# A decoder block on one core: the second FFN projection wholly by seven half-size products, with the sums of its weights begun earlier and the last row's squares summed on VectorE

## The chip, the cores and the metric

The kernel runs on one core of a Trainium2 chip. A core has five engines, each with its own instruction queue that is worked off in order: TensorE (PE; its weight loads are listed as PEld), VectorE (DVE), ScalarE (ACT), GpSimd (POOL) and SyncE (SP, which here only issues DMAs). They wait for each other by semaphores. Matmul results stand in eight PSUM banks of 128 partitions x 512 fp32 words. The metric is the device time of one launch in microseconds; lower is better.

## The reference

One layer of a decoder block, batch 1, 512 tokens, model width 1024, everything in fp32. The first half (a gated MLP mixer and a sparse attention, merged and projected) leaves the residual stream `x`; the change lies in the second half and the final norm:

```python
    h2 = rms_norm(x, norm2_g) * (1.0 + scale2) + shift2
    f_g, f_u = jnp.split(h2 @ w_ffn_in, 2, axis=-1)
    x = x + gate2 * ((jax.nn.silu(f_g) * f_u) @ w_ffn_out)
    return x
...
    return rms_norm(x, final_norm_g)
```

`w_ffn_out` is 2816 x 1024: 22 k tiles of 128 rows, two halves of 512 columns.

## The kernel before

**Precision.** An fp32 product is made of three fp32r matmuls (`mm3`, L51 to 55): each operand is split into `hi` (a rounded copy, made by ScalarE, L112 for weights and L1579 for activations) and `lo` (the rest, made by VectorE, L116 and L1583), and hi·hi, hi·lo and lo·hi are added in PSUM.

**Order.** The order of instructions on every engine is the order in which the program emits them. Weights come through one stream: SyncE loads a chunk into one of three `raw` buffers, `prep` splits it into one of three `hi`/`lo` pairs, and `get(i)` sees to it that the chunks up to two ahead are prepared before chunk i is used. So ScalarE's `hi` of chunk i+2 waits until TensorE is through with chunk i-1.

**Stages.** Towards the end of the span they are: projection B (`opt_b` over `W_PB`, eight chunks, with `o_step` called after each), the output projection O (`oprod`, seven half-size products, then direct matmuls over `W_O`), the second norm and its transposes, the first FFN projection (a direct part, then `sprod`, twenty rounds `q` of seven products), and the second FFN projection, which is what the change is about.

**The second FFN projection, called Z here.** Its output (512 x 1024) is four quadrants of 256 tokens x 512 columns, each in two PSUM banks (`Z[0]` to `Z[3]`). Twenty of the 22 k tiles are cut into two halves of ten (`KZ`) and done by Strassen's scheme in Winograd's form: seven products instead of eight, `zprod`, in the order A11, S1, S2, A12, S3, A22, S4. Each takes an activation operand (A.. are parts of the activations `gz`; S1 = A21-A22, S2 = A11-S1, S3 = S2-A22, S4 = A12-S2, formed in place by VectorE in `a_sum`, split by `a_hi` and `a_lo` into `za`) and a weight operand (quarters of `w_ffn_out`, or one of four sums of quarters, `wsum` 1 to 4). A product is five chunks of two k tiles: per chunk and per 128 tokens (`e`) six matmuls of 512 columns. The lists handed to `zprod` hold, for each chunk, the small jobs that are emitted between `get` and the chunk's matmuls. `z_copy` and `z_out` copy quadrants by ScalarE, `z_add` adds a kept copy by VectorE.

The two k tiles left over (`KC`, tiles 20 and 21) are added directly after the fifth product: their activations are split into `gs` (`g_hi`, `g_lo`, L1792 and L1795), and two chunks `W_FO` are multiplied into all four quadrants, 48 matmuls of 512 columns.

**The weight sums.** `wsum` 1 to 4 are made in DRAM by DMAs that GpSimd issues, some of them adding into their target (L305), some copying (L307). They are cut into five row chunks of six steps each, and the steps are dealt out by `wstep` (L317): a ScalarE copy and a GpSimd copy of one column (L323, L324) hold the step's DMAs back to that place, then they are issued, each after those before it on the same rows have landed. `wstep` is called twice in each of the twenty rounds q; every fourth call does nothing.

**The end.** During the last two products the finished quadrants are scaled by the gate, added to the residual and squared: `resid_v` (two VectorE passes, L1238 and L1239; ScalarE sums the squares, L1240), `scale_g` (VectorE, L1724), `row_rstd` (VectorE reduces, L1247, GpSimd raises to -1/2, L1248) and `finish` (scaling shared by VectorE and ScalarE, L1728 and L1727, then the store). The last product's third to fifth chunk are done for token tile 0 first and then for token tile 1 in two column halves, so that most of the end overlaps matmuls.

## Time and profile before

| | us |
|---|---|
| median of 3 runs | 823.71 (823.35 to 824.3) |
| the profiled execution | 824.09 |
| its span, first to last instruction | 822.3 |
| TensorE busy in the span | 807.8 |
| VectorE busy | 683.2 |
| ScalarE busy | 427.6 |
| GpSimd busy | 156.3 |

The granted TensorE clock was 0.998 of full speed in that execution. A matmul's listed duration is a modelled one that overlaps with the next matmul's; the pace at which matmuls are issued is read from the starts of many of them. Likewise two VectorE rows can overlap a little, so what one costs in a row of them is the distance of their starts.

### The profile page before, as it was taken

To read this page: it belongs to the slowest core of one execution; us is meant where nothing else is said; L and a number is where in the kernel's file an instruction comes from. 1 tells how busy PE (TensorE), PEld (TensorE's weight loads), DVE (VectorE), ACT (ScalarE), POOL (GpSimd) and SP (SyncE) were. 2 spreads that over 40 slices of the span, in tenths; PEclk is the share of its full clock that TensorE was granted. 3 is DMA by queue.
4 is the path that set the end of the run, shared out by engine and by line. 5 is a ranking of instruction groups with operands and counts; after the bars stand their busy time and mean duration, and the time that the engine had idled before them with its cause. 6 is when DMAs were issued, how large, how long until landed. Compare 5 with 4: busy or idle time off the path is not lost.

```text
span 822.3 us, 12898 instructions
## 1 busy us (share of the span) xinstructions
PE 807.8 (98%) x4912; PEld 721.2 (88%) x4912; DVE 683.2 (83%) x1163; ACT 427.6 (52%) x758; POOL 156.3 (19%) x171
## 2 busy tenths in 40 slices
...
GB/s 295 311 210 119 103 179 78 106 101 89 113 135 201 174 185 103 26 111 257 201 124 20 186 26 149 198 268 230 296 224 246 200 220 173 231 205 203 180 128 128
DMA packets 107197, 138.46 MB, mean 168 GB/s; under 512 B 6480, under 2 KB 77136, under 8 KB 106976
## 3 DMA queue, kind: packets, MB, share of 16 engines
...
q0 software_dynamic: 9584, 27.07, 14.1%
...
q10 hardware_dynamic: 720, 0.82, 0.3%
...
## 4 chain that ended last, share of the span: by engine, by line
PE 53%; DVE 17%; DMA 5%; ACT 2%; issue 2%; POOL 0%; POOLq 0%; DVEq 0%; ACTq 0%
PE R L53 8%; PE R L54 8%; PE R L55 8%; DMA mraw<-in_w_ada_dram 4%; DVE acc L177 3%; PE pfo L55 3%; PE pfo L54 3%; PE pfo L53 3%; DVE lo L116 2%; DVE sco L720 2%; DVE m L716 2%; PE pb L53 2%; PE pb L55 2%; PE pb L54 2%; PE po L54 2%
## 5 line engine op out<-in xcount | busy, mean ns | idle before, releaser
L112 ACT ACTIVATE hi<-raw 128x1024 fp32r<-128x1024 f32 (+2 forms) x103 | 107.0, 1040 | 107.7 <-PE pb L54 27.5
L116 DVE TENSOR_TENSOR lo<-raw,hi 128x1024 fp32r<-128x1024 f32 (+2 forms) x67 | 81.1, 1215 | 30.5 <-ACT hi L112 30.3
L116 POOL TENSOR_TENSOR lo<-raw,hi 128x1024 fp32r<-128x1024 f32 x29 | 73.2, 2529 | 127.9 <-ACT hi L112 122.2
L53 PE MATMUL pb<-h,hi 128*128 128x512 f32 (+1 forms) x192 | 74.6, 388 | 0.0
L55 PE MATMUL pb<-h,lo 128*128 128x512 f32 (+1 forms) x192 | 73.9, 385 | 0.0
L54 PE MATMUL pb<-h,hi 128*128 128x512 f32 (+1 forms) x192 | 73.9, 385 | 0.0
L54 PE MATMUL pfo<-lo,za 128*128 128x512 f32 (+1 forms) x146 | 56.5, 387 | 1.0 <-DVE lo L116 1.0
L55 PE MATMUL pfo<-hi,za 128*128 128x512 f32 (+1 forms) x146 | 56.2, 385 | 0.0
L53 PE MATMUL pfo<-hi,za 128*128 128x512 f32 (+1 forms) x146 | 56.2, 385 | 0.0
L177 DVE SCALAR_TENSOR_TENSOR acc<-mraw,cols,acc 128x512 f32<-128x512 f32 x49 | 40.1, 818 | 17.4 <-DMA mraw<-in_w_ada_dram 16.4
L53 PE MATMUL R<-tb,sx 128*128 128x256 f32 x160 | 45.2, 282 | 0.3 <-ACT R L1683 0.3
L1248 POOL TENSOR_TENSOR sm<-sm,mhalf 128x1 f32<-128x1 f32 x8 | 5.3, 663 | 209.8 <-DVE sm L1247 209.8
L54 PE MATMUL R<-tb,sx 128*128 128x256 f32 x160 | 45.1, 282 | 0.0
L55 PE MATMUL R<-tb,sx 128*128 128x256 f32 x160 | 45.0, 281 | 0.0
L55 PE MATMUL R<-tb,lo 128*128 128x256 f32 x160 | 44.8, 280 | 0.0
L53 PE MATMUL R<-tb,hi 128*128 128x256 f32 x160 | 44.8, 280 | 0.0
L54 PE MATMUL R<-tb,hi 128*128 128x256 f32 x160 | 44.6, 279 | 0.0
L55 PEld LDWEIGHTS pb<-h,lo 128*128 128x128 f32 x192 | 36.0, 188 | 7.3
L54 PEld LDWEIGHTS pb<-h,hi 128*128 128x128 f32 x192 | 36.0, 188 | 6.9
L53 PEld LDWEIGHTS pb<-h,hi 128*128 128x128 f32 x192 | 36.0, 188 | 6.9
L324 POOL COPY sm<-sm 128x1 f32<-128x1 f32 x30 | 18.9, 632 | 106.0 <-ACT sm L323 105.9
L54 PE MATMUL pav<-lo,h 128*128 128x256 f32 x128 | 35.8, 279 | 0.0
(380 smaller groups left out, 2666.7 us busy)
## 6 DMA issues: line engine op xcount, KB each, us to landing
...
```

Of the source, the lines that this page charges most:

```text
L53: T.matmul(o, wh, rh, start=start, stop=False, **kw)
L54: T.matmul(o, wh, rlo, start=False, stop=False, **kw)
L55: T.matmul(o, wlo, rh, start=False, stop=stop, **kw)
L112: A.activation(hi[:, :m], e["raw"][:, :m], AF.Copy)
L116: e["lo"].tensor_sub(lo[:, :m], e["raw"][:, :m], f(hi[:, :m]))
L177: V.scalar_tensor_tensor(o, w, cs[:, j:j + 1], o, op0=OP.mult, op1=OP.add)
L324: P.tensor_copy(t, t)
L716: V.max(m8s[i], sco[i])
L720: V.match_replace(out=sco[i], in_to_replace=m8s[i], in_values=sco[i], imm_value=TAKEN)
L1248: P.tensor_tensor(r2[:, tk:tk + 1], r2[:, tk:tk + 1], mhalf[:, :1], op=OP.pow)
```

## The change

All 22 k tiles of Z go through the seven products, in halves of eleven. A product is now five chunks of two k tiles and a sixth chunk of one (256 KB, half the columns to split, half the matmuls). The direct part (`W_FO`, `gs`) is gone. The operand parts for the sixth chunk are 128 x 256 pieces (`zl`, two places used in turn). The sums in DRAM have a sixth row chunk of half the size, so 36 steps in place of 30; eight calls of `wstep` are added ahead of the twenty rounds: five in the later `o_step` of projection B, three in O. `final_norm_g` is loaded into another buffer, its load emitted with the fifth product's first chunk instead of its last. At the end, three chunks (five k tiles) instead of three chunks of two are done in the split order. Row 0's scaling is done by ScalarE alone, and for the last quarter the squares are summed by VectorE in one pass that also adds the sums made before (GpSimd adds those up ahead of it).

```diff
--- before.py
+++ after.py
@@ -266,12 +266,11 @@
     W_F = [group(w_ffn_in, c, where=wh) for c in (0, DFF)]
     st["limit"] = len(stream)
 
-    KZ = ([0, 1, 2, 3, 4, 5, 6, 7, 12, 13], [8, 9, 10, 11, 16, 17, 18, 19, 14, 15])
-    KC = [20, 21]
-    NZ = 5
+    KZ = ([0, 1, 2, 3, 4, 5, 6, 7, 12, 13, 20], [8, 9, 10, 11, 16, 17, 18, 19, 14, 15, 21])
+    NZ = 6
 
     dram = ctx.enter_context(tc.tile_pool(name="dram", bufs=1, space=bass.MemoryType.DRAM))
-    wsum = {n: dram.tile([NZ * 256, 512], F32, name=f"wsum{n}") for n in (1, 2, 3, 4)}
+    wsum = {n: dram.tile([11 * 128, 512], F32, name=f"wsum{n}") for n in (1, 2, 3, 4)}
     W_Z = {}
 
     def add_z(key):
@@ -281,24 +280,22 @@
                 src, k0, c0 = wsum[key], 2 * c, 0
             else:
                 src, k0, c0 = w_ffn_out, KZ[key[0]][2 * c], key[1] * 512
-            W_Z[key].append(add_w(src, [k0, k0 + 1], c0, 512))
-
-    for key in ((0, 0), 1, 2, (1, 0), 3):
+            W_Z[key].append(add_w(src, [k0, k0 + 1][:1 + (c < 5)], c0, 512))
+
+    for key in ((0, 0), 1, 2, (1, 0), 3, 4, (1, 1)):
         add_z(key)
-    W_FO = [add_w(w_ffn_out, KC, 512 * h, 512) for h in range(2)]
-    for key in (4, (1, 1)):
-        add_z(key)
 
     def wsum_steps():
 
         def step(c, *moves):
-            o = slice(256 * c, 256 * c + 256)
+            n_ = 256 if c < 5 else 128
+            o = slice(256 * c, 256 * c + n_)
 
             def fn():
                 for n, add, src in moves:
                     if isinstance(src, tuple):
                         k = KZ[src[0]][2 * c] * 128
-                        src = w_ffn_out[k:k + 256, 512 * src[1]:512 * src[1] + 512]
+                        src = w_ffn_out[k:k + n_, 512 * src[1]:512 * src[1] + 512]
                     else:
                         src = wsum[src][o]
                     if add:
@@ -319,7 +316,8 @@
 
         fn = wsteps.pop(0) if wsteps else None
         if fn:
-            t = sm[:, 20 + len(wsteps):21 + len(wsteps)]
+            k = 20 + sum(w is not None for w in wsteps)
+            t = sm[:, k:k + 1]
             A.activation(t, cols[:, 58:59], AF.Copy)
             P.tensor_copy(t, t)
             fn()
@@ -1217,6 +1215,8 @@
     def o_step():
         for fn in O_STEPS.pop(0):
             fn()
+        if len(O_STEPS) < 5:
+            wstep()
 
     mbank[0] = 5
     o_issue("B11", "B12", "B22")
@@ -1404,15 +1404,18 @@
     o_m("S3")
     keep(O, 3, None)
     o_w("B22", "B22")
+    wstep()
     oprod(1, "S2", "T2", False)
     o_m("S4")
     o_sub("B11", "B21", "B11")
     seed(O, OB, 2, 1)
     oprod(0, "A12", "B21", False)
+    wstep()
     o_w("T4", "B11")
     o_m("A22")
     ensure(W_O[1])
     oprod(2, "S3", "T3", False)
+    wstep()
     keep(O, 2, "acc")
     oprod(1, "S4", "B22", False)
     ensure(W_O[2])
@@ -1550,7 +1553,7 @@
 
 
 
-    za = {}
+    za, zl = {}, []
     ZA = {"A11": ("S2_0", "E2", "F0"), "S1": ("E4", "S2_4", "S2_6"), "S2": ("E3", "E7", "S2_7"),
           "A12": ("E0", "E1", "S2_2"), "S3": ("S2_0", "E2", "F0"), "A22": ("E4", "S2_4", "S2_6"),
           "S4": ("E3", "E7", "S2_7")}
@@ -1560,14 +1563,20 @@
 
     def a_part(name, c):
         kh, th = AT_[name]
-        t = gz[((0, 1, 3), (2, 4, 3))[kh][c]]
-        if c == 2:
-            t = t[:, 2 * kh:2 * kh + 2]
+        t = gz[((0, 1, 3, 5), (2, 4, 3, 5))[kh][c]]
+        if c >= 2:
+            n = 4 - c
+            t = t[:, n * kh:n * kh + n]
         return t[:, :, th * 256:(th + 1) * 256]
 
     def a_hi(key, c):
-        h = ZA[key][c]
-        if c == 2:
+        h = (ZA[key] + (None,))[c]
+        if c == 3:
+            if not zl:
+                zl.append(base.tile([128, 2, 2, 1, 256], F32R, name="zl", tag="S2_3", bufs=1))
+            t = zl[0][:, ("A11", "S1", "S2", "A12", "S3", "A22", "S4").index(key) % 2]
+            t = (t[:, 0], t[:, 1])
+        elif c == 2:
             t = (base if h[0] == "S" else ffn[0]).tile([128, 2, 2, 256], F32R, name="za", tag=h, bufs=1)
             t = (t[:, 0], t[:, 1])
         elif h[0] == "S":
@@ -1733,12 +1742,12 @@
     Z, ZB = {}, ((4, 7), (0, 1), (2, 3), (5, 6))
 
     def zmm(o, ka, c, e, w, cc, start, stop):
-        ah, al = za[ka, c // 2]
+        ah, al = za[ka, c // 2 if c < 5 else 3]
         wh, wl = w
-        for j in range(2):
-            k_ = 2 * (c % 2) + j
+        for j in range(1 + (c < 5)):
+            k_ = 2 * (c % 2) + j if c < 5 else 0
             a = tuple(t[:, k_, e * 128:(e + 1) * 128] for t in (ah, al))
-            mm3(o, a, (wh[:, j, cc], wl[:, j, cc]), start and j == 0, stop and j == 1, skip_group_check=True)
+            mm3(o, a, (wh[:, j, cc], wl[:, j, cc]), start and j == 0, stop, skip_group_check=True)
 
     ALL = slice(0, 512)
 
@@ -1780,46 +1789,31 @@
         while left:
             left.pop(0)()
 
-    fng, gs = [], []
+    fng = []
 
     def load_fng():
-        fng.append(base.tile([128, D], F32, name="fng", tag="S2_3", bufs=1))
+        fng.append(ffn[0].tile([128, D], F32, name="fng", tag="E0", bufs=1))
         P.dma_start(fng[0], rows_bcast(final_norm_g, D))
 
-    def g_hi():
-        t = ffn[0].tile([128, 2, 2, S], F32R, name="gs", tag="E0", bufs=1)
-        gs.extend((t[:, 0], t[:, 1]))
-        A.activation(gs[0], gz[5], AF.Copy)
-
-    def g_lo():
-        V.tensor_sub(gs[1], gz[5], f(gs[0]))
-
-    zprod(0, "A11", (0, 0), True, [[outs_left, hi_("S1", 0)], [lo_("S1", 0), hi_("S1", 1)],
-                                   [lo_("S1", 1), hi_("S1", 2), sm_("S2", 1), lo_("S1", 2)],
-                                   [sm_("S2", 2), hi_("S2", 0)], [lo_("S2", 0), hi_("S2", 1)]])
+    zprod(0, "A11", (0, 0), True, [[outs_left, hi_("S1", 0)], [lo_("S1", 0), hi_("S1", 1), hi_("A11", 3)],
+                                   [lo_("S1", 1), lo_("A11", 3), hi_("S1", 2), sm_("S2", 1)],
+                                   [lo_("S1", 2), sm_("S1", 3), sm_("S2", 2), hi_("S2", 0)],
+                                   [sm_("S2", 3), lo_("S2", 0), hi_("S1", 3)], [lo_("S1", 3), hi_("S2", 1)]])
     z_copy(1, 0, -1.0)
-    zprod(3, "S1", 1, True, [[lo_("S2", 1), hi_("S2", 2), sm_("S4", 0), lo_("S2", 2)], [sm_("S4", 1), hi_("A12", 0)],
-                             [sm_("S4", 2), lo_("A12", 0)], [hi_("A12", 1)],
-                             [lo_("A12", 1), hi_("A12", 2)]])
+    zprod(3, "S1", 1, True, [[lo_("S2", 1), hi_("S2", 2), sm_("S4", 0)], [lo_("S2", 2), sm_("S4", 1)],
+                             [sm_("S4", 2), sm_("S4", 3), hi_("A12", 0)], [lo_("A12", 0), hi_("A12", 1)],
+                             [lo_("A12", 1), hi_("A12", 2)], [lo_("A12", 2)]])
     z_out(3)
-    zprod(1, "S2", 2, False, [[lo_("A12", 2), sm_("S3", 0)], [sm_("S3", 1)], [sm_("S3", 2), hi_("S3", 0)],
-                              [lo_("S3", 0), hi_("S3", 1)], [lo_("S3", 1), hi_("S3", 2)]])
+    zprod(1, "S2", 2, False, [[hi_("S2", 3), sm_("S3", 0)], [lo_("S2", 3), sm_("S3", 1)], [sm_("S3", 2), sm_("S3", 3)],
+                              [hi_("S3", 0)], [lo_("S3", 0), hi_("S3", 1)], [lo_("S3", 1), hi_("A12", 3)]])
     z_copy(2, 1, -1.0)
-    zprod(0, "A12", (1, 0), False, [[lo_("S3", 2), hi_("A22", 0)], [lo_("A22", 0), lambda: z_add(1, 3, V.tensor_add)],
-                                    [hi_("A22", 1)], [lo_("A22", 1), hi_("A22", 2)], [lo_("A22", 2)]])
-    zprod(2, "S3", 3, False, [[hi_("S4", 0)], [lo_("S4", 0), hi_("S4", 1)], [lo_("S4", 1), hi_("S4", 2)],
-                              [lo_("S4", 2), g_hi], [g_lo, load_fng]])
+    zprod(0, "A12", (1, 0), False, [[lo_("A12", 3), hi_("S3", 2)], [lo_("S3", 2), lambda: z_add(1, 3, V.tensor_add)],
+                                    [hi_("A22", 0)], [lo_("A22", 0), hi_("A22", 1)], [lo_("A22", 1), hi_("A22", 2)],
+                                    [lo_("A22", 2)]])
+    zprod(2, "S3", 3, False, [[hi_("S3", 3), load_fng], [lo_("S3", 3), hi_("S4", 0)], [lo_("S4", 0), hi_("S4", 1)],
+                              [lo_("S4", 1), hi_("S4", 2)], [lo_("S4", 2), hi_("A22", 3)], [lo_("A22", 3)]])
     z_out(2)
     z_add(3, 2, V.tensor_sub)
-
-
-    for h in range(2):
-        hi, lo = get(W_FO[h])
-        for tk in range(4):
-            o = (Z[h] if tk < 2 else Z[2 + h])[tk % 2]
-            for j in range(2):
-                mm3(o, tuple(t[:, j, tk * 128:(tk + 1) * 128] for t in gs), (hi[:, j], lo[:, j]), False, True,
-                    skip_group_check=True)
 
 
     sq = []
@@ -1834,16 +1828,16 @@
         while sq:
             sq.pop(0)()
 
-    zprod(2, "A22", 4, False, [[res_(0, 0)], [sq_, res_(1, 0)], [sq_, res_(2, 1)], [sq_, res_(3, 1)], [sq_]])
+    zprod(2, "A22", 4, False, [[res_(0, 0)], [sq_, res_(1, 0)], [sq_], [res_(2, 1)], [sq_, hi_("S4", 3)], [lo_("S4", 3)]])
 
     def done(tk):
         row_rstd(tk)
         finish(tk)
 
-    zprod(1, "S4", (1, 1), False, [[res_(2, 0)], [sq_, res_(3, 0)]])
+    zprod(1, "S4", (1, 1), False, [[res_(3, 1)], [sq_, res_(2, 0)], [sq_, res_(3, 0)]])
     last = bank(7, "pfo")
     A.activation(last[:, :256], Z[1][1][:, 256:], AF.Copy)
-    ids = W_Z[1, 1][2:]
+    ids = W_Z[1, 1][3:]
     ch = [get(i, 2 - k) for k, i in enumerate(ids)]
     sq_()
     done(2)
@@ -1853,7 +1847,7 @@
             c = ALL if z is None else slice(256 * z, 256 * z + 256)
             o = Z[1][0] if z is None else (Z[1][1][:, :256], last[:, :256])[z]
             for n_, w in enumerate(ch):
-                zmm(o, "S4", 2 + n_, tk, w, c, False, n_ == 2)
+                zmm(o, "S4", 3 + n_, tk, w, c, False, n_ == 2)
             n = c.stop - c.start
             if z is None:
                 resid(o, 512, 512, 1, tk, gate_b[2])
@@ -1861,11 +1855,19 @@
                 row_rstd(tk)
             elif z == 0:
                 resid(o, 512, n, 1, tk, gate_b[2])
-                finish(0)
+                scale_g(512, n, tk)
+                A.activation(xo[0], xo[0], AF.Copy, scale=r2[:, 0:1])
+                for c_, q in ((slice(0, 640), SY), (slice(640, 1024), A)):
+                    q.dma_start(out[0:128, c_], xo[0][:, c_])
+
+                P.tensor_scalar(ss2[:, tk, 3:4], ss2[:, tk, 1:2], ss2[:, tk, 0:1], EPS, op0=OP.add, op1=OP.add)
             else:
-                resid(o, 768, n, 2, tk, gate_b[2])
-                scale_g(512, n, tk)
-                row_rstd(tk)
+                resid_v(o, 768, n, 2, tk, gate_b[2])
+                c_ = slice(768, 768 + n)
+                V.tensor_tensor_reduce(out=t512("sq")[:, :n], in0=xt[tk][:, c_], in1=xt[tk][:, c_],
+                                       scale=1.0 / 1024, scalar=ss2[:, tk, 3:4], op0=OP.mult, op1=OP.add,
+                                       accum_out=ss2[:, tk, 2:3])
+                P.tensor_tensor(r2[:, tk:tk + 1], ss2[:, tk, 2:3], mhalf[:, :1], op=OP.pow)
                 scale_g(768, n, tk)
                 finish(tk)
```

## The prediction

> **What bounds the kernel now.** I read the page's line of engines first, then who makes TensorE wait from projection B on, then the starts of matmuls inside Z, then VectorE's timeline at Z's two ends. The first line is the page's (busy us, share, count), the others TensorE's waits from 380 us on (us in all, times, longest).
>
> ```profile
> PE 807.8 (98%) x4912; PEld 721.2 (88%) x4912; DVE 683.2 (83%) x1163; ACT 427.6 (52%) x758; POOL 156.3 (19%) x171
> ...
> PE pfo L54 <- DVE lo L116: 1.0, 3, 0.4
> PE R L53 <- ACT R L1683: 0.3, 1, 0.3
> PE pfo L55 <- DVE gs L1795: 0.3, 1, 0.3
> ```
>
> From 380 us to the end TensorE waits 1.6 us in all, and three of the five waits are for a weight's `lo` in Z. So the matmuls set the time, with VectorE close behind where its work is bunched. The pace of the matmuls, from the instructions of line 53 in two windows (first and last start behind the durations), and two rows of TensorE's timeline (start, us):
>
> ```profile
> L53 PE MATMUL pfo<-hi,za x79: 389/395/397, 719.6 to 773.8; 128*128 128x512 f32 x79
> ...
> L53 PE MATMUL pfo<-hi,za x12: 277/282/285, 810.4 to 814.3; 128*128 128x256 f32 x12
> ...
> 774.50 0.40 PE L53 MATMUL pfo<-hi,gs 128*128 128x512 f32 x1
> ...
> 786.25 0.40 PE L53 MATMUL pfo<-hi,za 128*128 128x512 f32 x1
> ```
>
> Every third matmul is on L53, so 512 columns take (773.8-719.6)/(78x3) = 0.232 us and 256 columns (814.3-810.4)/(11x3) = 0.118 us. The listed 395 ns is no cost. The direct part lies between the last two rows: 11.75 us for 48 matmuls, with one short wait.
>
> **TensorE's work.** Before: 7 x 5 x 12 = 420 matmuls of Z and 48 direct, of which 18 run as 36 halves; 450 and 36. After: 7 x 66 = 462, of which 15 run as 30 halves; 447 and 30. The saving is 3 x 0.232 + 6 x 0.118 = 1.4 us. That is all the arithmetic gives, and the question is whether VectorE lets it through. It gets more to do: per product a half-size weight `lo` and a 256-wide `lo`, and four more 256-wide sums; it loses two weight `lo`s and the `gs` one.
>
> **Z's first product (VectorE behind).** Two lines of the chain that ended last, then the timeline of VectorE and of TensorE (in brackets the idle time before, and who ended it):
>
> ```profile
> 699.02 7.94 DMA raw<-in_w_ffn_out_dram
> 706.98 1.07 ACT hi L112
> ...
> 708.07 1.23 DVE L116 TENSOR_TENSOR lo<-raw,hi 128x1024 fp32r<-128x1024 f32 x1 [5.99 <-ACT hi L112]
> 709.21 0.41 DVE L1658 TENSOR_TENSOR gq<-fs,R 128x256 f32<-128x256 f32 x1
> 709.54 0.42 DVE L1695 TENSOR_TENSOR gq<-R,ps 128x256 f32<-128x256 f32 x1
> ...
> 711.47 1.22 DVE L116 TENSOR_TENSOR lo<-raw,hi 128x1024 fp32r<-128x1024 f32 x1
> 712.60 1.22 DVE L1583 TENSOR_TENSOR za<-gq,za 128x1024 fp32r<-128x1024 f32 x1
> ...
> 717.14 0.69 DVE L1583 TENSOR_TENSOR za<-gq,za 128x512 fp32r<-128x512 f32 x1
> 717.75 1.22 DVE L116 TENSOR_TENSOR lo<-raw,hi 128x1024 fp32r<-128x1024 f32 x1
> ...
> 718.21 0.40 PE L53 MATMUL pfo<-hi,za 128*128 128x512 f32 x1
> 719.02 0.50 PE L54 MATMUL pfo<-lo,za 128*128 128x512 f32 x1 [0.41 <-DVE lo L116]
> ```
>
> A weight load that lands at 706.98 leaves VectorE idle for 6 us, and from 708.07 it runs without a gap. By the distances of starts a pass 1024 wide costs 1.13 to 1.14 us, 512 wide 0.60, 256 wide 0.34. Product S1's first weight `lo`, at 717.75, holds its first matmuls back: L54 runs at 719.02, due at 718.44.
>
> With the change, from 711.47 on VectorE has in front of that `lo` five passes 1024 wide (two weights, two operand `lo`s, one sum; 5.68), three 512 wide (the half-size weight, an operand `lo`, a sum; 1.80) and two 256 wide, both new (0.70): 8.2 us, so it starts at 719.65 and ends 1.22 later, at 720.87. TensorE could do L54 at 718.44 plus the sixth chunk's six matmuls, 719.8; it gets to at 720.9, and this wait grows from 0.6 to 1.1 us. Behind the waiting matmul stands all of TensorE's queue. Then VectorE gains again: by the same counting S1's second weight is ready 0.3 us early, later ones more.
>
> The unknown here is the landing. SyncE's three loads share the DMA engines with the weight sums:
>
> ```profile
> q0 software_dynamic: 47, 0.56, 22.0%
> ...
> q0 software_dynamic: 267, 0.52, 86.9%
> ...
> 698.67 0.52 POOL L307 DMA_DIRECT2D wsum<-wsum  x1 [3.77 <-DMA wsum<-in_w_ffn_out_dram]
> ...
> 705.07 0.87 POOL L305 DMA_DIRECT2D wsum<-in_w_ffn_out_dram  x1 [4.68 <-DMA wsum<-wsum]
> ```
>
> The first line is the share of GpSimd's queue from 699 to 707 us (22% of 8 us, 1.8 us of all engines), the second the same from 530 to 534 us, where one adding move ran nearly alone (3.5 us). The moves at this place are now half as large, so they land earlier and GpSimd, which waits for each (its bracketed waits), issues the next earlier: the adding half (1.7 us) comes out of its place behind the loads into their midst, while the copy may be over before them. If both halves fall within, landing is 0.6 us later; if neither does, up to 1.8 earlier. I take 0.2 earlier, toward the lower end, since the adding half almost surely falls within. The first wait moves with it one for one.
>
> **The middle.** S1, S2, A12 and S3 are 4 x 66 x 0.232 = 61.1 us with VectorE ahead (a product is 15.3 us of matmuls; the fullest list, S1's, is 14.1 us of passes at the prices above). Counted from 720.8, S3 ends at 781.9, less the 0.2.
>
> **Where the direct part was.** It also stood between S3 and A22, which both add into Z[2], while `z_out` copies it:
>
> ```profile
> 773.30 0.60 ACT L1764 ACTIVATE ps<-pfo 128x512 f32<-128x512 f32 x1 [0.34 <-PE pfo L55]
> ...
> 786.45 1.06 ACT L112 ACTIVATE hi<-raw 128x1024 fp32r<-128x1024 f32 x1 [4.54 <-PE pfo L55]
> ```
>
> With that cover gone A22's first matmul waits for the first copy. A `hi` starts 0.2 us into a chunk (786.45 against 786.25) and takes 1.06; S3's sixth chunk lasts 1.4, so ScalarE is free about when S3 ends, and its copy takes 0.6 and little lies over: a new wait of 0.5 us, from 0.2 if the copy slips in before the split to 1.0 if the sums hold ScalarE too. A22 starts at 782.4, 3.8 earlier than 786.25.
>
> **From A22 to the end (VectorE behind again).**
>
> ```profile
> 788.68 0.69 DVE L1238 TENSOR_TENSOR rt<-pfo,gate2b 128x512 f32<-128x512 f32 x1
> ...
> 790.74 1.22 DVE L116 TENSOR_TENSOR lo<-raw,hi 128x1024 fp32r<-128x1024 f32 x1
> ...
> 808.98 0.15 DVE L1247 TENSOR_REDUCE sm<-ss 128x1 f32<-128x5 f32 x1
> ...
> 811.58 0.68 DVE L1238 TENSOR_TENSOR rt<-pfo,gate2b 128x512 f32<-128x512 f32 x1
> ...
> 813.79 0.16 DVE L1247 TENSOR_REDUCE sm<-ss 128x1 f32<-128x5 f32 x1
> ...
> 815.12 0.42 DVE L1238 TENSOR_TENSOR rt<-pfo,gate2b 128x256 f32<-128x256 f32 x1
> ...
> 815.91 0.42 DVE L1724 TENSOR_TENSOR xo<-xr,fng 128x256 f32<-128x256 f32 x1
> ...
> 817.67 0.55 DVE L1728 TENSOR_SCALAR xo<-xo,sm 128x640 f32<-128x640 f32 x1 [0.44 <-POOL sm L1248]
> ```
>
> One finished quadrant tile costs VectorE 2.06 us (788.68 to 790.74), a weight 1.13. The new lists put two of them on A22's first two chunks, one on the fourth, and three on S4; VectorE idles in A22's fifth and sixth chunk. It starts its last stretch with S4's second weight, whose `hi` may begin when A22's fifth chunk is through: 60 x 0.232 = 13.9, 0.2 to start, 1.1 from `hi` to `lo` (706.98 to 708.07): 15.2 us after A22's start. From there: weight 1.13, operand 0.35, weight 1.13 (0.1 waited), tile 2.06, weight 1.13, tile 2.06, weight 1.13, tile 2.06, half weight 0.60 = 11.7, then as before 2.60 (808.98 to 811.58) and 2.21 (to 813.79). Row 0's reduction comes 31.7 us after A22's start, where it came 813.79-786.25 = 27.5. So it is 4.2-3.8 = 0.4 us later than before, less the 0.2. TensorE is done 30.9 after A22's start, with VectorE two us behind: here the matmuls no longer set the end.
>
> **The last quarter.** From that reduction to the final scaling it was 817.67-813.79 = 3.88. The 640-wide scaling of row 0 leaves VectorE; the 256-wide `scale_g` moves ahead of z1; ScalarE's squares with their two hand-overs (815.91 past the reduction) become one VectorE pass. A like pass (maximum in place of sum) is in the attention:
>
> ```profile
> L1042 DVE CUSTOM_DVE_ANT_0 pt<-qk,sco 128x256 f32<-128x256 f32 x8 | 3.0, 417 | 0.0
> L1042 DVE DVE_READ_ACCUMULATOR2_ANT mx<- 128x1 f32 x32 | 2.7, 83 | 0.0
> ...
> 816.98 0.66 POOL L1248 TENSOR_TENSOR sm<-sm,mhalf 128x1 f32<-128x1 f32 x1 [2.40 <-DVE sm L1247]
> ```
>
> The new chain on VectorE: the reduction (0.07), gate and add of the first half (0.79, as 815.12 to 815.91), `scale_g` (0.34), gate and add of the second half (0.79), the squares (0.34 and 0.08 for the read), then GpSimd's power (0.66, and 0.1 around it): 3.2, a gain of 0.7. Bounds: 0.2 if the pass costs twice, 1.0 if GpSimd is quick.
>
> [...]
>
> **The moved sums.** Six steps run in projection B and O: eight DMAs of 512 KB, six ScalarE and six GpSimd copies of one column.
>
> ```profile
> 468.05 1.41 POOL L1248 TENSOR_TENSOR sm<-sm,mhalf 128x1 f32<-128x1 f32 x2 [86.99 <-DVE sm L1247]
> ...
> 457.11 1.06 ACT L112 ACTIVATE wx<-raw 128x1024 fp32r<-128x1024 f32 x1 [0.26 <-DMA raw<-in_w_ffn_in_dram]
> ...
> 485.55 1.15 ACT L1260 ACTIVATE xn<-xr,sm 128x1024 f32<-128x1024 f32 x1 [1.29 <-POOL sm L1248]
> ...
> 487.05 0.38 PE L1282 MATMUL x2T<-cst,xn 128*128 128x128 f32 x2
> ```
>
> GpSimd stands idle for the 87 us before the second norm, so a wait there holds nobody, and no step of Z waited for a sum. I cost the move at 0; the price if the cover fails is the second rival's.
>
> **Sum.** -0.5: +0.4 (VectorE's two stretches against TensorE's shorter work) -0.2 (landing) -0.7 (last quarter). The profiled execution took 824.09, 0.4 above the median; on the median 823.71 that makes 823.2.
>
> **Rivals.** *VectorE keeps up* (chance 0.27). If the late load lands over a microsecond earlier, the first wait goes, and where the last stretch packs closer than I count, the matmuls set the end: -1.4 for them, -1.0 for the old `lo` waits, -0.7 for the last quarter, +0.2 for the new wait over the `gs` one: 820.8. For it: VectorE idles 6 us ahead of 708.07. Against: its stretches were gapless before and are longer now.
>
> *The sums slow O's weight loads* (0.14). The fifth and sixth step's moves meet the loads for the rows at 457.11, which waits for its load already. One adding move is 3.5 us of all DMA engines; ScalarE's `xn` at 485.55 ends at 486.70, 0.35 ahead of the transposes that TensorE begins at 487.05. What delay stops TensorE lies between these 0.35 and 0.35 plus the 1.29 that ScalarE idles just there; I take 1.3, near the upper end, because the loads' rows come 28 us ahead. The whole 3.5 then costs 2.2: 825.4.
>
> *The landing is later* (0.07). Both halves fall among the loads, 0.6 later where I took 0.2 earlier: 824.0. It decides the first stretch alone; the last one starts from TensorE.
>
> *The forecast* (0.52), own range 822.0 to 824.6: the landing's bounds are cut short by TensorE on the early side (0.6 of waits to lose there), and the others are 0.5 each.
>
> **Chances.** About 0.2%, 1.65 us, is what a measurement of this kernel can tell from none. Faster by more: the first rival and the forecast's edge, 0.30. Slower by more: the second and as much of an edge, 0.18. Within: 0.52. The range over all cases, 820.7 to 825.3, leaves out the first rival's full sum's better half and the second's worse one.
>
> **What would show it.** Right: VectorE gapless from the late `lo` to S1's second product, a wait of about 1 us at S1's start, a 0.5 us one on ScalarE at A22's start, TensorE done two us ahead of VectorE's last quarter, no TensorE wait from 390 to 500 us. Wrong: TensorE waiting at 475 to 490 us, or none at S1's start, or a last quarter over 3.9 us.

## The result, and the profile after

The kernel after the change takes 826.5 us (median of 9 runs, 825.06 to 828.39), the kernel before 823.71 (9 runs, 823.05 to 825.04): a ratio of 1.0035, 95% interval 1.0023 to 1.0048. The forecast was 823.2 with a range to 825.3, so the change costs 2.8 us where it was to save 0.5. The profiled execution took 826.5 with a span of 824.7 us, 2.4 longer than that of before.

Who made TensorE wait in the kernel after, from 370 us on (us in all, times, longest), in answer to the list of before:

```profile
PE pf L53 <- ACT h L1290: 1.5, 1, 1.5
PE x2T L1282 <- ACT xn L1260: 0.6, 1, 0.6
PE pf L54 <- DVE h L1291: 0.6, 2, 0.3
PE R L53 <- ACT R L1692: 0.3, 1, 0.3
PE pfo L53 <- ACT ps L1773: 0.3, 1, 0.3
PE pfo L54 <- DVE lo L116: 0.2, 1, 0.2
```

The waits for a weight's `lo` in Z have nearly gone (1.0 us before, 0.2 now), and the list is led by waits that had not been there: on the normed activations `xn` and `h`, around the second norm, 220 us ahead of the projection that was changed. The starts of O, of the rounds and of Z come from TensorE's timeline. Before:

```profile
435.18 0.39 PE L53 MATMUL po<-ow,om 128*128 128x512 f32 x1
...
503.00 0.29 PE L53 MATMUL R<-h,sa 128*128 128x256 f32 x1
...
703.69 0.40 PE L53 MATMUL pfo<-hi,za 128*128 128x512 f32 x1
```

and after, with the first matmul of A22, the sixth product (start and duration in us, the idle time ahead of it in brackets):

```profile
435.13 0.39 PE L53 MATMUL po<-ow,om 128*128 128x512 f32 x1
...
506.94 0.28 PE L53 MATMUL R<-h,sa 128*128 128x256 f32 x1
...
707.64 0.40 PE L53 MATMUL pfo<-hi,za 128*128 128x512 f32 x1
...
784.50 0.50 PE L53 MATMUL pfo<-hi,za 128*128 128x512 f32 x1 [0.27 <-ACT ps L1773]
```

VectorE's last rows of after:

```profile
816.15 0.16 DVE L1247 TENSOR_REDUCE sm<-ss 128x1 f32<-128x5 f32 x1
816.22 0.41 DVE L1238 TENSOR_TENSOR rt<-pfo,gate2b 128x256 f32<-128x256 f32 x1
...
817.13 0.42 DVE L1733 TENSOR_TENSOR xo<-xr,fng 128x256 f32<-128x256 f32 x1
817.47 0.42 DVE L1238 TENSOR_TENSOR rt<-pfo,gate2b 128x256 f32<-128x256 f32 x1
...
818.49 0.48 DVE L1867 CUSTOM_DVE_ANT_0 sq<-xr,ss 128x256 f32<-128x256 f32 x1
818.90 0.08 DVE L1867 DVE_READ_ACCUMULATOR2_ANT ss<- 128x1 f32 x1
...
819.77 0.55 DVE L1737 TENSOR_SCALAR xo<-xo,sm 128x640 f32<-128x640 f32 x1 [0.45 <-POOL sm L1870]
```

Cut at these rows, the two spans compare so (us; the forecast's column holds what the prediction gave for the stretch):

| stretch | before | after | forecast | measured |
|---|---|---|---|---|
| up to O's first matmul | 435.18 | 435.13 | 0 | -0.05 |
| O to the rounds' first matmul | 67.82 | 71.81 | 0 | **+3.99** |
| the rounds | 200.69 | 200.70 | 0 | 0 |
| Z's start to A22's start | 82.56 | 76.86 | -4.0 | -5.7 |
| A22's start to row 0's reduction | 27.54 | 31.65 | +4.2 | +4.1 |
| reduction to final scaling | 3.88 | 3.62 | -0.7 | -0.26 |
| final scaling to the span's end | 4.6 | 4.9 | 0 | +0.3 |
| sum | | | -0.5 | +2.4 |

The changed projection did somewhat better than forecast. All of the loss, and more, lies in O, where the change put three calls of `wstep` and which I had costed at nothing.

**What happened in O.** ScalarE's timeline, before, where it splits O's and the first FFN projection's weights (the rows of line 112; 457.11 stands in the prediction):

```profile
449.89 1.05 ACT L112 ACTIVATE wx<-raw 128x1024 fp32r<-128x1024 f32 x1
453.57 1.06 ACT L112 ACTIVATE wx<-raw 128x1024 fp32r<-128x1024 f32 x1 [2.62 <-DMA raw<-in_w_out_dram]
```

The same after, with GpSimd's and SyncE's rows of those microseconds ahead of it:

```profile
447.99 0.88 POOL L302 DMA_DIRECT2D wsum<-in_w_ffn_out_dram  x1 [2.47 <-DMA wsum<-wsum]
...
449.59 0.37 SPq L92 DMA_DIRECT2D raw<-in_w_out_dram  x1
450.72 13.01 SPq L92 DMA_DIRECT2D raw<-in_w_ffn_in_dram  x4
...
449.84 1.06 ACT L112 ACTIVATE wx<-raw 128x1024 fp32r<-128x1024 f32 x1
458.69 1.06 ACT L112 ACTIVATE wx<-raw 128x1024 fp32r<-128x1024 f32 x1 [7.79 <-DMA raw<-in_w_out_dram]
...
461.44 1.06 ACT L112 ACTIVATE wx<-raw 128x1024 fp32r<-128x1024 f32 x1 [0.23 <-DMA raw<-in_w_ffn_in_dram]
```

and what the DMA queues moved from 450 to 453 us (packets, MB, share of the 16 engines), first after, then before:

```profile
q0 software_dynamic: 229, 0.46, 105.5%
q1 hardware_dynamic: 5, 0.01, 2.3%
```

```profile
q1 hardware_dynamic: 324, 0.58, 60.4%
```

The sixth early step's adding move goes out at 447.99, held until then by the landing of the copying move before it. 1.6 us later SyncE asks for O's last weight, and then for more. The packets of GpSimd's queue q0 took 105.5% of the 16 engines' time, and SyncE's q1 had 5 packets of the 234 in these three microseconds. The weight that ScalarE split at 453.57, it splits at 458.69; counted from O's first matmul that is 23.56 in place of 18.39 us, 5.2 later. SyncE had two more loads out by then, and q1 moved 1.4 MB from 453 to 458 us, so the three came in close together. Everything behind it (residual, squares, norm, transposes) is 4 to 5 us later too (ScalarE's first squares start at 465.83 in place of 460.80), until TensorE stands still at the norm. The listed waits there make 2.7 of the 3.99; the rest is not listed as a wait.

### The profile page after: what moved, and what is told of

Same layout as the page of the kernel before. It is cut to its first block, busy times and chain, and to the rows that moved or that the text cites. A ratio compares the mean times of both kernels' runs of the same rounds, so it can differ in the third digit from the quotient of the medians.

```text
span 824.7 us, 12949 instructions
## 1 busy us (share of the span) xinstructions
PE 807.0 (98%) x4903; PEld 719.9 (87%) x4903; DVE 687.3 (83%) x1178; ACT 431.3 (52%) x773; POOL 165.7 (20%) x186
## 4 chain that ended last, share of the span: by engine, by line
PE 86%; DVE 4%; DMA 3%; ACT 3%; issue 2%; SPq 1%; POOL 0%; POOLq 0%; DVEq 0%; ACTq 0%
PE pb L55 9%; PE pb L53 9%; PE pb L54 9%; PE R L53 8%; PE R L54 8%; PE R L55 8%; PE pfo L53 4%; PE pfo L55 4%; PE pfo L54 4%; PE pav L54 2%; PE pav L53 2%; PE pav L55 2%; PE pgb L53 2%; PE pgb L54 2%; PE pgb L55 2%; DMA s<-in_w_ada_dram 2%
## 5 line engine op out<-in xcount | busy, mean ns | idle before, releaser
L112 ACT ACTIVATE hi<-raw 128x1024 fp32r<-128x1024 f32 (+2 forms) x108 | 109.3, 1013 | 104.0 <-PE pb L54 38.5
L116 DVE TENSOR_TENSOR lo<-raw,hi 128x1024 fp32r<-128x1024 f32 (+2 forms) x72 | 83.5, 1163 | 24.2 <-ACT hi L112 23.9
L322 POOL COPY sm<-sm 128x1 f32<-128x1 f32 x36 | 23.6, 656 | 178.7 <-ACT sm L321 178.7
L53 PE MATMUL pav<-hi,h 128*128 128x256 f32 x128 | 35.7, 279 | 0.0
```

The lines of the kernel that those rows point to most:

```text
L53: T.matmul(o, wh, rh, start=start, stop=False, **kw)
L112: A.activation(hi[:, :m], e["raw"][:, :m], AF.Copy)
L116: e["lo"].tensor_sub(lo[:, :m], e["raw"][:, :m], f(hi[:, :m]))
L322: P.tensor_copy(t, t)
```

## The experiments

The theory after these readings: **A**, one adding move in the middle of O keeps O's weight loads waiting. Its rivals: the one-column copies that come with each step, the greater number of sums in the rounds, any place near weight loads, the new end. Times are medians; the kernel before ran beside each group at 823.5 to 823.8. All lines of the records are counted from O's first matmul where it helps, because the time up to there differs by up to 1.8 us between executions.

### Where the early steps stand: e1, e2, e3

e1 is the kernel after with all 36 steps dealt out in the rounds; the calls in `o_step` and O are gone:

```diff
-        return [fn for k in range(0, len(order), 3) for fn in order[k:k + 3] + [None]]
+        return [fn for k in range(0, len(order), 9) for fn in order[k:k + 9] + [None]]
...
-        if len(O_STEPS) < 5:
-            wstep()
...
     o_w("B22", "B22")
-    wstep()
...
     oprod(0, "A12", "B21", False)
-    wstep()
...
     oprod(2, "S3", "T3", False)
-    wstep()
```

> The changed kernel with all 36 steps of the weight sums back in the twenty rounds (every tenth call of wstep does nothing, instead of every fourth). Theory A (an adding move in O keeps the DMA engines from O's last weight loads, and TensorE waits 4.0 us at 474 to 486 us): those waits are gone, and the time is 826.5 - 4.0 = 822.5, or up to 824.5 if the steps, which now follow each other more closely, still run when Z begins. Theory B (where the sums run is of no matter; the loss is Z's fuller VectorE and the end): 826.5 within 0.5, with the waits at 474 to 486 us as they are.

e2 is the other way round: the kernel before, with six of its 30 steps moved to projection B and O; the others stay at their places.

```diff
-        return [fn for k in range(0, len(order), 3) for fn in order[k:k + 3] + [None]]
+        seq = [fn for k in range(0, len(order), 3) for fn in order[k:k + 3] + [None]]
+        return seq[:8] + [None] * 8 + seq[8:]
...
         for fn in O_STEPS.pop(0):
             fn()
+        if len(O_STEPS) < 5:
+            wstep()
...
     o_w("B22", "B22")
+    wstep()
...
     oprod(0, "A12", "B21", False)
+    wstep()
...
     oprod(2, "S3", "T3", False)
+    wstep()
```

> The kernel before with its first six steps alone moved to where the changed kernel has them, in projection B and O; its other steps stay at their places in the rounds. Theory A: 823.7 + 4.0 = 827.7, with TensorE's waits at 474 to 486 us. Theory B: 823.7 within 0.5.

e3 is the kernel after with the three calls in O taken out alone; its steps run in the rounds, in place of calls that did nothing.

```diff
-        return [fn for k in range(0, len(order), 3) for fn in order[k:k + 3] + [None]]
+        seq = [fn for k in range(0, len(order), 3) for fn in order[k:k + 3] + [None]]
+        return [fn for k, fn in enumerate(seq) if k not in (7, 11, 15)]
...
     o_w("B22", "B22")
-    wstep()
...
     oprod(0, "A12", "B21", False)
-    wstep()
...
     oprod(2, "S3", "T3", False)
-    wstep()
```

> The changed kernel without the three calls of wstep in O: four steps stay in projection B, and the two that O had come first in the rounds (three idle calls are dropped for them). Theory A: it is O's last step that meets the loads, so the waits at 474 to 486 us go, 826.5 - 4.0 = 822.5. Theory C (the doubled moves in projection B already delay what O needs): the waits stay for the most part, above 825.

Measured: e1 824.71 (822.67 to 828.92, 12 runs; ratio to before 1.0023, 1.0007 to 1.0038), e2 825.25 (824.29 to 826.95; 1.0020, 1.0012 to 1.0029), e3 823.93 (822.57 to 827.59; 1.0011, 1.0000 to 1.0023). The stretch from O's first matmul to the rounds takes 67.82 us in e1 and 67.94 in e3, as before the change, and 69.90 in e2, which has the steps. e2 lost 2.08 us there and not the 4.0 expected of it: the same move made O's last weight 3.2 us late in place of 5.2, as the table below shows; why is open. So the early steps, and nothing else of the change, bring the loss in O. e1 and e3 do not win it all back in every run; the rounds' new waits are taken up below.

### The copies or the DMAs, adding or copying: e7, e8, e9

e7 is e3 with the two steps' one-column copies, without their DMAs, left in O:

```diff
     o_w("B22", "B22")
+    A.activation(sm[:, 60:61], cols[:, 58:59], AF.Copy)
+    P.tensor_copy(sm[:, 60:61], sm[:, 60:61])
...
     oprod(0, "A12", "B21", False)
+    A.activation(sm[:, 61:62], cols[:, 58:59], AF.Copy)
+    P.tensor_copy(sm[:, 61:62], sm[:, 61:62])
```

> The kernel after with the two steps' one-column copies on ScalarE and GpSimd left in O, but without their DMAs (these steps are dealt out in the rounds). Theory A (the DMAs alone cost): no wait over 0.3 us between 474 and 491, the rounds start near 503.2, time as with no step in O, 823.9. Rival M (the one-column copies hold up ScalarE or GpSimd): the waits on h (1.5) and xn (0.6) stay, rounds start near 507, time 826.5.

e8 is the kernel after, with the sixth early move copying where it added, which leaves a bare quarter in the first row chunk of `wsum` 4, so that its output is another:

```diff
-            ((4, 0, 2),), ((4, 1, (1, 0)),))] for c in range(NZ)]
+            ((4, 0, 2),), ((4, int(c > 0), (1, 0)),))] for c in range(NZ)]
```

> The kernel after with the sixth early step's move copying instead of adding (wsum 4 then holds a bare quarter in its first row chunk, so the output differs). Theory A with its price (an adding move of 512 KB takes 3.5 us of all engines, a copying one about 1.3): SyncE's loads behind it land about 2 us earlier than after the change, TensorE's wait on h falls from 1.5 to 0.5 or none, the rounds start at 504 to 505 instead of 506.94, time 824.3. Rival (any move at that place holds SyncE's loads back, whatever its length): rounds start at 506.5 or later, time 826.5.

e9 is the kernel after, with that one step moved to an idle call early in the rounds; the copying step stays in O:

```diff
-        return [fn for k in range(0, len(order), 3) for fn in order[k:k + 3] + [None]]
+        seq = [fn for k in range(0, len(order), 3) for fn in order[k:k + 3] + [None]]
+        seq[6], seq[11] = None, seq[6]
+        return seq
```

> The kernel after with one step moved: the sixth (the adding move that in O's middle holds SyncE's loads back) goes from O into the first rounds, into a call that did nothing. Everything else, the copying step in O too, stays. Theory A (this one adding move at this place is the whole loss): no TensorE wait over 0.3 us between 474 and 491, the rounds start at 503 to 504, time 823.5 (the copying variant gave 823.6), that is 3 under the kernel after. Rival: the adding move meets loads in the rounds as well, the loss comes back there as waits on R or ps, time 825 or more.

Measured: e7 823.47 (822.62 to 827.44; ratio 1.0006, 0.9993 to 1.0018), e8 823.62 (822.94 to 826.72; 1.0001, 0.9991 to 1.0011), e9 822.81 (822.31 to 823.74; 0.9993, 0.9984 to 1.0002). One adding move out of 36 steps, put elsewhere or made a copying one, takes the kernel after from 826.5 to 822.8 or 823.6. The one-column copies cost nothing: e7 needs 67.82 us from O to the rounds. All of e9's waits on TensorE from 370 us on:

```profile
PE R L53 <- ACT R L1694: 0.3, 1, 0.3
PE pfo L53 <- ACT ps L1775: 0.3, 1, 0.3
PE pfo L54 <- DVE lo L116: 0.2, 1, 0.2
```

Nothing is left between 474 and 491 us. The four variants also give the price. The split of O's last weight, from ScalarE's timeline of e8 and then of e2:

```profile
455.52 1.06 ACT L112 ACTIVATE wx<-raw 128x1024 fp32r<-128x1024 f32 x1 [4.23 <-DMA raw<-in_w_out_dram]
```

```profile
456.68 1.06 ACT L112 ACTIVATE wx<-raw 128x1024 fp32r<-128x1024 f32 x1 [5.53 <-DMA raw<-in_w_out_dram]
```

| | split, from O's start | late by | O to the rounds | lost | covered |
|---|---|---|---|---|---|
| before | 18.39 | | 67.82 | | |
| e8, copying move | 20.00 | 1.61 | 68.27 | 0.45 | 1.16 |
| e2, adding move | 21.62 | 3.23 | 69.90 | 2.08 | 1.15 |
| after, adding move | 23.56 | 5.17 | 71.81 | 3.99 | 1.18 |

O's first matmul is at 435.18, 435.52, 435.06 and 435.13. In these three runs, whatever the delay, 1.15 to 1.18 us of it is hidden and the rest goes one for one into the time.

### The last two steps in projection B: e5

```diff
         for fn in O_STEPS.pop(0):
             fn()
-        if len(O_STEPS) < 5:
-            wstep()
+        wstep()
```

with O's three calls gone as in e3.

> The kernel after with all six early steps in projection B (every one of its eight o_step calls, the steps' order unchanged) and none in O. Theory A (the adding move of the sixth step takes the DMA engines for some 3 us just when SyncE loads O's and the first FFN projection's weights, and everything from there runs 4 us late): the waits on h and xn between 474 and 491 us go, matmuls of the rounds start near 503.0 as before the change, the rounds stay at 200.7 us because no step is added to them, and the time falls by about 4 to 822.5. Rival B (any place near a stream of weight loads is as bad): the waits turn up in projection B instead, on a weight's hi or lo, and the time stays at 825 to 827. Rival C (what costs is the longer queue of sums in the rounds): 825 or more with the waits in the rounds.

827.1 (826.58 to 827.58; ratio 1.0041, 1.0027 to 1.0054): rival B, no better than O. Two of TensorE's waits in e5, a row of VectorE's timeline and one of GpSimd's:

```profile
PE pb L55 <- DVE lo L116: 1.3, 1, 1.3
PE po L53 <- ACT po L1374: 0.8, 1, 0.8
```

```profile
417.78 1.54 DVE L177 SCALAR_TENSOR_TENSOR acc<-mraw,cols,acc 128x512 f32<-128x512 f32 x2 [5.66 <-DMA mraw<-in_w_ada_dram]
```

```profile
435.88 0.88 POOL L302 DMA_DIRECT2D wsum<-in_w_ffn_out_dram  x1 [0.39 <-DMA wsum<-wsum]
```

1.3 us are lost in B itself. VectorE waited there 5.7 us for a load of `mraw` (1.5 in the kernel after), while GpSimd's adding moves of 405.61 and 406.74 ran: from 410 to 415 us q0 moved 381 packets and q1 130. VectorE's passes are still late in O (the one on line 1203 starts 5.2 us after O's start, 2.2 in the kernel after), and O to the rounds is 69.93, 2.1 more. The sixth step, though emitted in B, goes out only at 435.88, behind ScalarE's one-column copy at 435.06, which came late too. O lost nothing to it that shows: from 434 to 446 us q1 moved 7 packets, so no load of SyncE's stood behind it. A call's place in the program is only the earliest place of its move.

### Every time, or once: e14

The kernel after, unchanged, once more.

> The kernel after, unchanged, another execution. Theory A (the adding move in O costs the same every time): the rounds start within 0.5 of 506.9, the load stall lies at 450 to 461, the first residual pass near 464.4 instead of 459.4, and the last quarter is 3.6. Rival (O's loss is of the one execution): the rounds start at 503 to 505.

828.13 in this one run: O to the rounds takes 72.05, against 71.81, and in e4, the same kernel up to Z's end, 72.24. The loss came in all three executions. The delay is smaller in these two: O's last weight is split 23.09 and 23.14 us after O's start, 4.7 and 4.8 late, so by the table 3.5 and 3.6 would be lost, where 4.2 and 4.4 are. The 0.7 and 0.8 more come with a lower granted clock (0.61 in e4 in the stretch below). TensorE's busy time in two stretches (us, busy of PE, PEld, DVE, ACT, POOL, then the granted clock, DMA share, GB/s), first after, then e14:

```profile
482.00:486.00 4.00, 3.71 (x30) 3.31 (x29) 3.60 (x6) 3.94 (x8) 0.00 (x0) 1.00 0.00 0
```

```profile
482.00:486.00 4.00, 4.00 (x24) 4.00 (x23) 3.61 (x6) 3.94 (x9) 0.00 (x0) 0.57 0.00 0
```

Right behind its wait for `h`, TensorE in e14 had a mean granted clock of 0.57 over these four us, where the kernel after had 1.00: 24 matmuls in 4.00 busy us, against 30 in 3.71. The listed waits don't show this. Most of what else e14 is longer by lies in the rounds, 201.76 us in place of 200.70, with a wait of 0.8 on `R`; its cause was not followed up.

### The rounds: what e1 and e7 lost in some runs

In the profiled run of e7 (826.18) the rounds take 203.67 us in place of 200.7. Two of TensorE's waits in that stretch, and GpSimd's and SyncE's rows ahead of them:

```profile
PE R L53 <- ACT ps L1701: 1.6, 1, 1.6
PE R L53 <- ACT R L1681: 0.9, 1, 0.9
```

```profile
564.97 0.91 POOL L302 DMA_DIRECT2D wsum<-in_w_ffn_out_dram  x1 [9.30 <-DMA wsum<-in_w_ffn_out_dram]
...
561.52 2.18 SPq L1312 DMA_DIRECT2D raw<-in_w_ffn_in_dram  x2
```

In e9 the same pair of adding moves went out at 555.34:

```profile
555.34 1.83 POOL L302 DMA_DIRECT2D wsum<-in_w_ffn_out_dram  x2 [0.30 <-issue]
```

e7, which has one step more to do in the rounds, was 9.6 us behind with its moves at this place, and an adding move went out behind SyncE's two loads of the round's weights, which were still under way. It looks like the collision of O in the other order: from 565 to 568 us q1 moved 888 packets and q0 12, from 569 to 573 q0 387 and q1 111, and VectorE waited 3.2 us for a load. No run tests it. In e1's profiled run (828.92) the rounds take 204.2, with 2.8 us of such waits, and Z has 1.7 us of waits for a `lo`. That the other long runs of e1, e3 and e7 are of this kind is likely, but only these two were seen.

### The new end and VectorE's last stretch: e4, e10, e12

e4 is the kernel after with the end of before (ScalarE's squares, row 0's scaling shared by both engines).

```diff
-                scale_g(512, n, tk)
-                A.activation(xo[0], xo[0], AF.Copy, scale=r2[:, 0:1])
...
-                P.tensor_scalar(ss2[:, tk, 3:4], ss2[:, tk, 1:2], ss2[:, tk, 0:1], EPS, op0=OP.add, op1=OP.add)
+                finish(0)
             else:
-                resid_v(o, 768, n, 2, tk, gate_b[2])
...
+                resid(o, 768, n, 2, tk, gate_b[2])
+                scale_g(512, n, tk)
+                row_rstd(tk)
                 scale_g(768, n, tk)
```

> The changed kernel with the end as it was before: row 0 scaled by VectorE and ScalarE, the last squares by ScalarE. By the two traces the new end takes 0.3 us off the chain to the last scaling and gives 0.3 back in the last store: 826.5 within 0.4. If the end as forecast had gained 0.7: 827.2. If the new end costs, below 826.0.

826.69 (825.97 to 828.67): the new end is worth no more in the time than can be told. In the records row 0's reduction to the final scaling is 3.89 with the old end and 3.62 with the new.

e10 is e9 with the third chunk of the first product loaded once (it is asked for twice, in the kernel before too) and with VectorE's work for two finished quadrant tiles taken from A22 into S3, one from S4 into A22:

```diff
-        if q == NQ - 1:
-            issue(W_Z[0, 0][2])
...
-                              [lo_("S4", 1), hi_("S4", 2)], [lo_("S4", 2), hi_("A22", 3)], [lo_("A22", 3)]])
+                              [lo_("S4", 0), res_(0, 0), hi_("S4", 1)], [lo_("S4", 1), sq_, hi_("S4", 2)],
+                              [lo_("S4", 2), res_(1, 0), hi_("A22", 3)], [lo_("A22", 3), sq_]])
...
-    zprod(2, "A22", 4, False, [[res_(0, 0)], [sq_, res_(1, 0)], [sq_], [res_(2, 1)], [sq_, hi_("S4", 3)], [lo_("S4", 3)]])
+    zprod(2, "A22", 4, False, [[res_(2, 1)], [sq_, lambda: (scale_g(0, 512, 0), scale_g(0, 512, 1))], [res_(3, 1)],
+                               [sq_], [hi_("S4", 3)], [lo_("S4", 3)]])
...
-    zprod(1, "S4", (1, 1), False, [[res_(3, 1)], [sq_, res_(2, 0)], [sq_, res_(3, 0)]])
+    zprod(1, "S4", (1, 1), False, [[res_(2, 0)], [sq_, res_(3, 0)], [sq_]])
```

> e9 with two more edits: the first product's third chunk is loaded once instead of twice, and two of the six finished quadrant tiles move from the A22 product up into S3 (their scaling by final_norm_g stays in A22), a third from S4 into A22, so that VectorE's gapless last stretch is 2.06 us shorter. Theory V (VectorE, not the matmuls, sets the end: A22's start to row 0's reduction is 31.7 us where the matmuls take 30.9): row 0's reduction comes 1.2 to 2 us earlier counted from A22's start, the time is 0.8 to 2 below e9, 821.5 to 822.7, under the kernel before. Rival (the matmuls or the store set the end, VectorE's stretch only fills their shade): the same time as e9, 823.5.

822.6 (821.95 to 824.43; ratio 0.9990, 0.9981 to 0.9999), 0.2 under e9. The stretch from A22 to row 0's reduction fell from 31.65 to 30.15, but a wait ate the gain. TensorE's longest wait in e10, and ScalarE's rows there:

```profile
PE pfo L53 <- ACT ps L1773: 1.8, 1, 1.8
```

```profile
780.84 0.63 ACT L1242 ACTIVATE rt<-xr 128x512 f32<-128x512 f32 x1 [0.72 <-DVE xr L1241]
...
781.47 1.06 ACT L1773 ACTIVATE ps<-pfo 128x512 f32<-128x512 f32 x2
```

The squares of the tile that was moved up wait for VectorE, and the two copies of Z[2], for which A22 waits, stand behind them on ScalarE. e12 mends that and reduces rows 2 and 3 before it scales either:

```diff
-                              [lo_("S4", 2), res_(1, 0), hi_("A22", 3)], [lo_("A22", 3), sq_]])
+                              [lo_("S4", 2), res_(1, 0), hi_("A22", 3)], [lo_("A22", 3)]])
...
-    zprod(2, "A22", 4, False, [[res_(2, 1)], [sq_, lambda: (scale_g(0, 512, 0), scale_g(0, 512, 1))], [res_(3, 1)],
+    zprod(2, "A22", 4, False, [[sq_, res_(2, 1)], [sq_, lambda: (scale_g(0, 512, 0), scale_g(0, 512, 1))], [res_(3, 1)],
...
-    done(2)
-    done(3)
+    row_rstd(2)
+    row_rstd(3)
+    finish(2)
+    finish(3)
```

> e10 with two edits of order: the second moved tile's squares come on ScalarE behind the two copies of Z[2] instead of ahead of them, and the rows 2 and 3 are both reduced before either is scaled. In e10 A22's first matmul waited 1.8 us for these copies, behind the squares, and VectorE stood 0.68 us twice for GpSimd's power. Theory V (from A22 on VectorE sets the end, its start is A22's): the wait at A22's start falls back to 0.3, row 0's reduction comes 1.5 plus some 0.6 us earlier, time 820.2 to 821.2 against e10's 822.6. Rival (the store and the matmuls set the end): no more than the 1.5 of the wait in the records and less than 0.7 in the time, 822 or more.

820.49 (819.93 to 820.85, 5 runs; ratio 0.9963, 0.9950 to 0.9977): faster than both kernels, by 0.4% of before. A22's start and the reduction in e12:

```profile
780.08 0.50 PE L53 MATMUL pfo<-hi,za 128*128 128x512 f32 x1 [0.32 <-ACT ps L1773]
...
809.57 0.16 DVE L1249 TENSOR_REDUCE sm<-ss 128x1 f32<-128x5 f32 x1
```

29.49 us, 2.16 less than in the kernel after and in e9. So theory V holds: VectorE's row of passes from A22 on did set the end.

### Z's first product: e6, e11, e13, e15, e16, e17

The forecast had a weight split 3.3 us after Z's start, as before, and a wait behind it. After the change it is split 1.2 ahead of Z's start, and the wait is not there:

```profile
706.41 1.06 ACT L112 ACTIVATE hi<-raw 128x1024 fp32r<-128x1024 f32 x1 [1.05 <-DMA raw<-in_w_ffn_out_dram]
```

These runs ask why. e6 (and e16, the same kernel again) is the kernel before with the third chunk loaded once:

```diff
-        if q == NQ - 1:
-            issue(W_Z[0, 0][2])
```

> The kernel before without the second load of the first product's third chunk (it is loaded twice, once by the stream and once by an explicit call in the last round). My prediction held that the first product's late weight, which lands 3.3 us after Z's start, costs some 0.6 to 1.6 us of TensorE's waits (its listed waits for a weight's lo in Z are 1.0). Theory L (the landing sets these waits): one load less in the midst of the weight sums, the late one lands 1 to 2 us earlier, VectorE's idle of 6 us shrinks by as much, the lo waits of 1.0 fall to 0.3 or none, time 822.7 to 823.2. Rival (the matmuls hide it, or the engines just carry another load): 823.5 with the same waits.

> The kernel of e6 (before, the third chunk loaded once) in another execution. In e6 the adding move ahead of the first product's loads went out 14.86 us before Z's start, in three executions of the kernel before at 12.94, 13.02 and 13.09, though the program up to there is the same. Theory R (chance around an edge): between 12.9 and 14.9, split of the late weight before or after Z's start accordingly. Theory D (the double load sets it): 14.8 to 14.9 again.

e11 is e9 with the half-size rows of the sums second, so that the moves at the end of the rounds are full-size as before:

```diff
-            ((4, 0, 2),), ((4, 1, (1, 0)),))] for c in range(NZ)]
+            ((4, 0, 2),), ((4, 1, (1, 0)),))] for c in (0, 5, 1, 2, 3, 4)]
```

> e9 with the half-size row chunk of the sums second instead of last, so that the moves at the end of the rounds are full-size as in the kernel before. My prediction had the first product's late weight land about 3.1 us after Z's start and VectorE hold up the next product's first weight lo by 1.1 us; in the kernel after it landed before Z's start and the wait did not come. Theory H (the half-size moves at the end let the load land early): here it lands 2.5 to 3.5 us after Z's start as in the kernel before, the lo wait at the second product's start is 0.8 to 1.3, and Z's start to A22's start is 78 to 78.7 us instead of 76.9; time about 1.3 over e9, 824.8. Rival (the landing moved for another reason, such as the steps ending earlier): landing before Z's start, 76.9, time as e9.

e13 and e15 are the kernel before in two more executions, and e17 is it with longer sums:

```diff
-    wsum = {n: dram.tile([NZ * 256, 512], F32, name=f"wsum{n}") for n in (1, 2, 3, 4)}
+    wsum = {n: dram.tile([11 * 128, 512], F32, name=f"wsum{n}") for n in (1, 2, 3, 4)}
```

> The kernel before, unchanged, another execution. My first stretch rested on one execution in which the first product's late weight was split at 706.98, 3.3 us after Z's start, because a weight sum's adding move went out 0.5 us ahead of SyncE's load. Theory R (that lateness is of the one execution: the moves' chain drifts by 2 us from run to run): here the move goes out 14 to 15 us ahead of Z's start instead of 12.9, the split comes before or within 1 us after Z's start, and the lo waits in Z are under 0.6. Rival (it is the kernel's): again near 3.3 after Z's start, with about 1.0 of lo waits.

> The kernel before, unchanged, a third execution, for the same question as the second: Theory R gives an early split again or one in between, the rival 3.3 us after Z's start in all three.

> The kernel before with its four DRAM sums declared 1408 rows long, as after, instead of 1280; nothing else. Theory P (where the sums lie in DRAM sets how fast the moves are): the adding move goes out 14.6 to 14.9 us before Z's start and the late weight is split before or less than 1 us after Z's start. Rival: 12.9 to 13.1 and 3.0 to 3.3 after, as in the three executions of before.

e6 takes 823.22 (822.79 to 824.25; ratio 0.9993, 0.9984 to 1.0002), e11 823.12 (821.98 to 823.62; 0.9991, 0.9982 to 1.0000), not to be told from e9. The single runs of e13, e15, e16 and e17 lie at 823.43, 823.71, 823.57 and 823.68. What differs is when an adding move leaves, against the load that SyncE issues 12.4 us ahead of Z's start in every one of these records:

| | adding move, ahead of Z's start | late split, against Z's start |
|---|---|---|
| before, e13, e15 | 12.95, 13.02, 13.09 | 3.3, 3.1, 3.0 after |
| e17 | 13.6 | 2.3 after |
| e11 | 14.6 | 0.8 ahead |
| after, e9 | 14.8, 14.9 | 1.2, 1.3 ahead |

The split of e13 and that of e11 (Z starts at 703.20 and 704.85) on ScalarE:

```profile
706.30 1.06 ACT L112 ACTIVATE hi<-raw 128x1024 fp32r<-128x1024 f32 x1 [5.38 <-DMA raw<-in_w_ffn_out_dram]
```

```profile
704.01 1.06 ACT L112 ACTIVATE hi<-raw 128x1024 fp32r<-128x1024 f32 x1 [1.44 <-DMA raw<-in_w_ffn_out_dram]
```

Where the adding move left 0.5 to 0.7 us ahead of the load (before, e13, e15), the split came 3.0 to 3.3 us after Z's start; where it left 2.2 us ahead (e11), 0.8 us before it. The lateness is the kernel's, since it came in all three executions of before (rival of e13), yet the half-size moves are not needed to end it (e11's rival). e17 fits neither its theory nor its rival. What holds the move back stands in GpSimd's rows, before and after:

```profile
690.74 0.88 POOL L305 DMA_DIRECT2D wsum<-in_w_ffn_out_dram  x1 [1.85 <-DMA wsum<-wsum]
```

```profile
692.80 0.80 POOL L302 DMA_DIRECT2D wsum<-in_w_ffn_out_dram  x1
```

In the kernel before, and in e13, e15, e16 and e17, it waited 1.1 to 1.9 us for the copying move ahead of it to land; where it goes out 14.8 or 14.9 ahead it waited for no landing. e2, the kernel before with its six early steps, has it at 14.9 too, with the split 0.7 after Z's start and `lo` waits of 0.3. So steps begun earlier are enough to bring the load in earlier. They are not the only way: the one-load kernel, without early steps, had the move at 14.9 and 13.7 in its two executions, so the distance also drifts by a microsecond from run to run. TensorE's waits for a `lo` in Z are 1.0, 0.7 and 0.7 us in the three executions of before and 0.3 in e2, e6, e16 and e17: of the listed waits this much, and no more, hung on the landing.

## Why the prediction was wrong, point by point

**The moved sums, the step that failed.** "GpSimd stands idle for the 87 us before the second norm, so a wait there holds nobody, and no step of Z waited for a sum. I cost the move at 0." It looked for who waits for GpSimd's engine and for the sums, and not for who shares the DMA engines with them. It cost 3.99 of a span that grew 2.4; with the one adding move elsewhere (e9) the time is 822.8, inside the forecast's own range. That it lies there is in part luck: Z's first product came 1.65 us better than forecast, the last quarter and the store 0.7 worse. Two of the prediction's own signs of being wrong came: TensorE's waits at 475 to 490 us, and none at S1's start.

**The rival that named it** had the mechanism, the place and the cover right: 0.35 to 1.64 with 1.3 taken, 1.15 to 1.18 measured. Mis-sized was the delay. I priced it as the move's own length, 3.5; the weight came 5.2 late. The loads that had piled up behind the move came in together (the first and the last of the three are split at 458.69 and 461.44), which fits, but in e2 they came in so too and the weight was 3.2 late: the size of the delay stays open. So 4.0 was lost instead of 2.2. Its chance was too low as well: the prediction names nothing against it but the cover of a microsecond, and the split at 457.11 already waited for its load.

**TensorE's arithmetic** was right. Z's start to A22's is five products of 66 matmuls at 0.232, 76.6, plus the listed wait of 0.3; measured 76.86.

**Z's first product** was wrong on the good side: no wait in place of 1.1, 1.65 us better than forecast. The step is the landing: "I take 0.2 earlier, toward the lower end", with 1.8 earlier as the bound. Against Z's start it came 4.5 earlier. I priced the two moves from 698.67 on; what counted was the adding move ahead of them, at 690.74, half a microsecond before SyncE's load of 691.28. Behind it the next load could be issued 5.1 us ahead of Z's start; after the change it is 7.5. So the first half of the rival *VectorE keeps up* came true. Its second half, a last stretch that packs closer, did not.

**A22's new wait** came as forecast (0.5; the matmul before it started at 783.84, so 784.50 is 0.43 late by the pace), and so did **VectorE's last stretch** (31.7 forecast, 31.65 measured), with TensorE's last matmul two microseconds ahead of VectorE's last passes (815.49 against 817.47). e12 shows that stretch to be the bound.

**The last quarter** gained 0.26, not 0.7. The passes here that read what the pass ahead of them wrote (816.67, 817.13, 817.92, 818.49) start 0.45 to 0.57 behind it, and I had taken 0.34 for every second one: 816.22 to 817.13 is 0.91, 817.47 to 818.49 is 1.02, each put at 0.79. The power took 0.87 from 818.90 to 819.77 where I had 0.76. GpSimd's addition of the sums was no part of that:

```profile
817.74 0.31 POOL L1863 TENSOR_SCALAR ss<-ss 128x1 f32<-128x1 f32 x1 [0.81 <-ACT rt L1240]
```

It ended at 818.05, 0.44 ahead of the squares that read it. The pass at 817.92 (L1239) beside it started 0.45 after the one ahead of it, like the one at 815.57 in the kernel before, beside which GpSimd ran nothing, so no wait shows here; but the two overlap by 0.13 us only.

**The store** is 0.3 longer, from the final scaling to the end. e4, with the old end, has the same 4.9 to 5.0, so it is not the new end; what it is was not tried.
